# Two blocks of mixed layers on one core: both parts of x in one 512-column matmul

## The chip, the core and the metric

The kernel runs on one core of one Trainium2 chip. The metric is the device time of one execution in microseconds, the median of several runs. TensorE multiplies, VectorE (DVE), ScalarE (ACT) and GpSimd (POOL) do the rest, and SyncE (SP) issues the transfers from HBM.

## What is computed

Four layers over 256 tokens of 2048 features in float32. Each layer is a norm, a wide projection in, a token mixer, and a projection out that is added to the residual. Cut to what matters here:

```python
def even_layer(x, ...):                     # first block: attention beside S5
    proj = rmsnorm(x, norm_g) @ w_in        # 2048 -> 6144
    q, k, v, u, z_a, z_b = split(proj)
    o_a = chunked_relpos_attention(q, k, v, rel_bias) * silu(z_a)
    y = gelu(s5_ssm(u, ...))                # a recurrence over tokens, 64 groups
    o_b = y * sigmoid(y @ w_glu + b_glu) * silu(z_b)
    return x + concatenate([o_a, o_b]) @ w_out
def odd_layer(x, ...):                      # attention with forget gates
    q, k, v, z, f = split(rmsnorm(x, norm_g) @ w_in)
    return x + (forgetting_attention(q, k, v, f) * silu(z)) @ w_out
# second block, even layer: HGRN2 beside sparse attention, its two halves
# joined @ w_out (4096 -> 2048); odd layer: a short convolution and a gated
# linear recurrence of 2560 features; a norm at the end of each block
```

Nearly all the arithmetic is the products with the weights. They are made from float32 numbers that are each cut in two parts, a rounded one ("hi") and the rest ("lo"): x·w is taken as hi·hi + hi·lo + lo·hi.

## The kernel before, in words

**Stream of weights.** `Kern.run` (line 267) walks over a list of jobs. A job is 1024 columns of weights in one tile: `issue` (276) has SP load it (`raw`, 512 KB, five buffers), `prep` (285) has ACT round it to `hi` and DVE take `lo` = raw − hi (four buffers each), and the job's matmuls follow on TensorE. `ahead` (313) splits the weights of the next two jobs before a job's matmuls are written down.

**Groups.** `Kern.group` (359) makes the jobs of 512 output features. In the orientation 'W' a job holds two blocks of 128 input features (k-tiles) and all 512 columns. For each k-tile and each of its four blocks of 128 columns it emits three matmuls through `mmr` (line 420), each with a weight load of its own, into one 256-column sum (256 tokens):

```python
self.mmr(o_, wh, xh, s, False)
self.mmr(o_, wh, xl, False, False)
self.mmr(o_, wl, xh, False, l)
```

So a job is 8 such triples, 24 matmuls. The four sums of a group fill a PSUM tile of 1024 columns; there are two such tiles (`ps_main`). In the orientation 'X' (the values of the attentions) x is the stationary side and the matmuls have 512 columns. `Act` (27) holds x for four k-tiles; `Act.split` (37) writes its hi and lo parts into two slots of 1024 columns, by one ACT and one DVE operation (or four of 256 columns each where a gain is multiplied in).

**What follows a group.** `post` functions empty the sums: `evac_scaled` multiplies by the norm's factor straight out of PSUM, `Layer.take` (1259) and `post_oa` add the sums of a projection out to the residual by one DVE operation of 1024 columns and split the result for the next layer. A `post` is put in `delayed` after its group's last matmul and written down in the next `bg_step`.

**Order of the work.** Everything that is not the weight stream (S5, the attentions, HGRN2, the norms) is written as generators in lanes. `bg_step` (234) lets each lane write down a step after each job, as long as a plan of the engines' busy time (`busy`, costs in `_ew`, `act`, `mm`; 2600 ns of clock for each job) says that no engine is over 3 us behind. Where a job needs something that is not yet written down, `run` calls `bg_step(force=True)` until it is: the steps then stand in the engines' queues with no job in between. Each engine works off its queue in order.

**The two places named below.** In the first layer (E1), `block(b)` in `s5` does the S5 recurrence for 8 blocks, two at a time: products into banks (bu), rotations and scans on DVE with two additions on POOL, the products of the outputs (y), the gelu, and after the fourth block of a half the split of `y[0]` or `y[1]`. The GLU's groups read `y[0]` in their first k-tiles and `y[1]` in their last. In the second block's even layer (E2) the 16 sparse attention heads end in `gate` (a POOL multiplication of 1024 columns) and the split of the last input of the projection out.

Of the kernel before, what the change touches and what calls it, by code (L numbers as in the profile page):

```python
# [26 lines left out]
class Act:  # L27
    """256 columns of tokens for `n` blocks of 128 features, as two float32r parts."""

    def __init__(self, K, src=None, n=4, scale=None, ready=False):  # L30
        self.K, self.src, self.n, self.scale, self.ready = K, src, n, scale, ready
        self.hi = self.lo = None
        self.uses = 0
        self.keep_src = False
        self.hook = None

    def split(self):
        if self.hi is not None:
            return
        assert self.ready  # L40
        K = self.K
        self.hi, self.lo = K.slot(F32R), K.slot(F32R)
        v = lambda t: t[:, :self.n * 256]
        if self.scale is None or isinstance(self.scale, float):
            sc = 1.0 if self.scale is None else self.scale
            K.act(v(self.hi), v(self.src), AF.Copy, scale=sc)
            if sc == 1.0:
                K.tt('D', v(self.lo), v(self.src), v(self.hi).bitcast(F32), OP.subtract)
            else:
                K.stt(v(self.lo), v(self.src), sc, v(self.hi).bitcast(F32), OP.mult, OP.subtract)  # L50
        else:
            for k in range(self.n):
                s = slice(k * 256, k * 256 + 256)
                K.act(self.hi[:, s], self.src[:, s], AF.Copy, scale=self.scale[:, k:k + 1])
                K.stt(self.lo[:, s], self.src[:, s], self.scale[:, k:k + 1],
                      self.hi[:, s].bitcast(F32), OP.mult, OP.subtract)
        if self.hook is not None:
            self.hook(self.src)
        if not self.keep_src:
            K.free_slot(self.src)  # L60
            self.src = None

    def used(self):
        self.uses -= 1
        if self.uses == 0:
            self.K.free_slot(self.hi)
            self.K.free_slot(self.lo)
            self.hi = self.lo = None


class Kern:
# [124 lines left out]
    def smax(self, out, a, b, acc):  # L196
        """out = -(a + b); acc = its least, the negative of the greatest of a + b"""
# [29 lines left out]
    def lane(self, gens, width=1, prio=0, name=""):  # L227
        """a queue of (condition, generator maker), `width` of them at a time"""
# [5 lines left out]
    def bg_step(self, force=False):  # L234
# [32 lines left out]
    def run(self):  # L267
        jobs = self.jobs
        units = []
        for j in jobs:  # L270
            units.append([(j['unit'][0][:, j['off']:j['off'] + j['n']], j['n']), None])
# [41 lines left out]
        def ahead(i):  # L313
            """the splits of the jobs after job i, as far as LOOK goes"""
# [44 lines left out]
    def group(self, name, src, acts, orient, post, units, ready=None, bg=False):  # L359
        """one group of 512 columns: `units` is the list of (DRAM AP, kt count)"""  # L360
        st = {}

        def ps():
            if 'ps' not in st:
                self.nslot += 1
                if bg:
                    self.banks.free -= 2
                    st['ps'] = [self.ps_bg.tile([128, 512], F32, name=f"b{self.nslot}{i}", tag="b") for i in range(2)]
                    st['half'] = st['ps']
                else:  # L370
                    p = st['ps'] = self.ps_main.tile([128, 1024], F32, name=f"mm{self.nslot}", tag="mm")
                    st['half'] = [p[:, :512], p[:, 512:]]
            return st['half']

        kt = 0
        total = sum(n for _, n in units)
        for u, n in units:
            key = (u, n * 512)
            for h in range(0, n, self.JK):
                w = min(self.JK, n - h)  # L380
                ks = list(range(kt + h, kt + h + w))
                al = []
                for k in ks:
                    if acts[k][0] not in al:
                        al.append(acts[k][0])
                for a in al:
                    a.uses += 1

                def mmf(hi, lo, ks=ks):
                    p = ps()  # L390
                    hv = hi.rearrange("p (k c) -> p k c", c=512)
                    lv = lo.rearrange("p (k c) -> p k c", c=512)
                    for i, k in enumerate(ks):
                        a, o = acts[k]
                        xh, xl = a.hi[:, o * 256:o * 256 + 256], a.lo[:, o * 256:o * 256 + 256]
                        f, l = k == 0, k == total - 1
                        if orient == 'W':
# [2008 lines left out]
```

## Time and profile before

| | |
|---|---|
| median of 3 runs | 2397.28 us (2393.36 to 2397.49) |
| span of the profiled execution | 2394.8 us (the page gives no other time of it) |
| PE busy, matmuls | 2336.9 us, 98% of the span, 19906 |
| weight loads busy | 2253.3 us, 94% |
| DVE busy | 1585.9 us, 66% |
| ACT busy | 1152.5 us, 48% |
| POOL busy | 386.8 us, 16% |
| DMA | 402 MB, 168 GB/s on average |

Busy time of PE is the time in which at least one matmul is in flight; matmuls overlap, so the pace is read from the starts of matmuls that follow each other, not from one matmul's length. The page's 40 slices show PE at nine tenths or more in all but the first and last, and the granted clock at its full 2.4 GHz but for a few short stretches. A "product" with two or three small matmuls of a lane on tile `b` stands at L219 or L224, those of the weight stream at L420; L165, L176 and L194 are helpers that record DVE operations, L214 records all of ACT.

### The profile page before, as it was taken

To read this page: it belongs to the slowest core of one execution; us is meant where nothing else is said; L and a number is where in the kernel's file an instruction comes from. 1 tells how busy PE (TensorE), PEld (TensorE's weight loads), DVE (VectorE), ACT (ScalarE), POOL (GpSimd) and SP (SyncE) were. 2 spreads that over 40 slices of the span, in tenths; PEclk is the share of its full clock that TensorE was granted. 3 is DMA by queue.
4 is the path that set the end of the run, shared out by engine and by line. 5 is a ranking of instruction groups with operands and counts; after the bars stand their busy time and mean duration, and the time that the engine had idled before them with its cause. 6 is when DMAs were issued, how large, how long until landed. Compare 5 with 4: busy or idle time off the path is not lost.

```text
span 2394.8 us, 47663 instructions
## 1 busy us (share of the span) xinstructions
PE 2336.9 (98%) x19906; PEld 2253.3 (94%) x19906; DVE 1585.9 (66%) x2409; ACT 1152.5 (48%) x1662; POOL 386.8 (16%) x320
## 2 busy tenths in 40 slices
PE   7999999999999999999999999999999999999997
PEld 7989998999999999989999999899999999999997
DVE  7978878675554545676758574566667446777764
ACT  5354454444444344543445443455555434666643
POOL 1111211010000000123324253101110000111210
PEclk9999999999999999999999999999999999999999
DMA  6544454555545555554544454554444555555453
GB/s 225 191 152 149 142 177 153 175 186 164 193 160 175 174 170 185 169 177 156 170 160 159 162 165 159 192 178 142 142 142 143 195 183 180 165 175 168 161 196 111
DMA packets 116167, 402.23 MB, mean 168 GB/s; under 512 B 14832, under 2 KB 17776, under 8 KB 115952
## 3 DMA queue, kind: packets, MB, share of 16 engines
q1 hardware_dynamic: 115952, 399.19, 50.7%
q8 instruction: 156, 2.56, 0.4%
q14 instruction: 59, 0.48, 0.1%
HBM read 396.00 MB, written 2.10 MB: 166 GB/s over the span
## 4 chain that ended last, share of the span: by engine, by line
PE 84%; DVE 8%; POOL 2%; issue 2%; ACT 2%; DMA 1%; DVEq 0%; SPq 0%; ACTq 0%; POOLq 0%
PE mm L420 75%; PE b L219 6%; DVE lo L165 3%; DVE s L165 2%; POOL s L165 2%; DVE s L194 1%; DVE s L176 1%; PE b L224 1%; PE b L420 1%; ACT s L214 1%; ACT hi L214 1%; DMA raw<-in_e_in 1%; PE b L1836 0%; DVE s L170 0%; DMA s<-in_e_bias 0%
## 5 line engine op out<-in xcount | busy, mean ns | idle before, releaser
L420 PE MATMUL mm<-s,hi 128*128 128x256 f32 x9984 | 1830.5, 285 | 10.4 <-ACT s L214 7.6
L420 PEld LDWEIGHTS mm<-s,hi 128*128 128x128 f32 x9984 | 1563.9, 193 | 18.3 <-ACT s L214 8.0
L420 PE MATMUL mm<-s,lo 128*128 128x256 f32 x4992 | 1418.6, 284 | 24.5 <-DVE lo L165 24.4
L165 DVE TENSOR_TENSOR lo<-raw,hi 128x1024 fp32r<-128x1024 f32 x730 | 934.0, 1294 | 622.2 <-ACT hi L214 620.4
L214 ACT ACTIVATE hi<-raw 128x1024 fp32r<-128x1024 f32 x730 | 756.9, 1054 | 646.1 <-PE mm L420 557.5
L420 PEld LDWEIGHTS mm<-s,lo 128*128 128x128 f32 x4992 | 960.8, 192 | 28.9 <-DVE lo L165 28.8
L165 POOL TENSOR_TENSOR s<-s,s 128x512 f32<-128x512 f32 (+1 forms) x128 | 273.9, 2154 | 1411.4 <-ACT s L214 586.9
L214 ACT ACTIVATE s<-s 128x1024 f32<-128x1024 f32 (+6 forms) x188 | 132.9, 713 | 263.3 <-DVE s L165 137.2
L420 PE MATMUL mm<-hi,s 128*128 128x512 f32 x768 | 244.6, 394 | 0.0
L219 PE MATMUL b<-s,s 128*32 128x32 f32 (+8 forms) x3008 | 175.0, 244 | 4.8 <-POOL s L186 2.1
L420 PEld LDWEIGHTS mm<-hi,s 128*128 128x128 f32 x768 | 145.0, 189 | 30.8 <-ACT s L214 0.3
L219 PEld LDWEIGHTS b<-s,s 128*32 128x32 f32 (+2 forms) x2976 | 148.3, 135 | 23.4 <-POOL s L186 2.5
L420 PE MATMUL mm<-lo,s 128*128 128x512 f32 x384 | 150.5, 392 | 1.6 <-DVE lo L165 1.6
L214 ACT ACTIVATE s<-b 128x384 f32<-128x384 f32 (+6 forms) x135 | 57.2, 462 | 134.9 <-PE b L219 92.7
L165 DVE TENSOR_TENSOR s<-s,s 128x512 f32<-128x512 f32 (+8 forms) x134 | 85.8, 666 | 45.7 <-ACT s L214 44.5
L420 PEld LDWEIGHTS mm<-lo,s 128*128 128x128 f32 x384 | 72.6, 189 | 16.7 <-DVE lo L165 2.4
L176 DVE SCALAR_TENSOR_TENSOR s<-s,s 128x1024 f32<-128x1024 f32 (+3 forms) x76 | 82.6, 1089 | 3.1 <-ACT s L214 2.2
L214 ACT ACT_TABLE_LOAD x44 | 56.5, 1283 | 16.1 <-DVE s L176 14.7
L204 DVE COPY_PREDICATED s<-hmask,b 32x64 f32<-32x64 int32 (+1 forms) x144 | 36.0, 250 | 30.4 <-PE b L219 26.6
L214 ACT ACTIVATE s<-s,nsam 128x15 f32<-128x15 f32 (+2 forms) x96 | 37.6, 394 | 36.0 <-DVE nsam L199 36.0
L170 POOL TENSOR_SCALAR s<-alibi 128x256 f32<-128x256 f32 x16 | 17.8, 1111 | 212.3 <-PE b L219 174.1
L186 POOL MEMSET s<- 128x512 f32 (+7 forms) x65 | 25.8, 410 | 123.3 <-DMA s<-in_e_bias 59.1
(148 smaller groups left out, 966.6 us busy)
## 6 DMA issues: line engine op xcount, KB each, us to landing
raw<-in_e_in SPq DMA_DIRECT2D x336, 512.0 KB, 4.1
raw<-in_o_in SPq DMA_DIRECT2D x208, 512.0 KB, 4.0
raw<-in_e_out SPq DMA_DIRECT2D x80, 512.0 KB, 4.2
raw<-in_o_out SPq DMA_DIRECT2D x72, 512.0 KB, 4.4
raw<-in_e_outa SPq DMA_DIRECT2D x16, 512.0 KB, 3.6
raw<-in_o_rg SPq DMA_DIRECT2D x10, 512.0 KB, 3.7
raw<-in_e_glu SPq DMA_DIRECT2D x8, 512.0 KB, 3.8
raw<-in_e_cmp SPq DMA_DIRECT2D x8, 512.0 KB, 5.1
```

What stands on the lines that cost most here:

```text
L165: self._eng(e).tensor_tensor(out, a, b, op=op)
L170: self._eng(e).tensor_scalar(out, a, s1, None, op0=op0)
L176: self.nc.vector.scalar_tensor_tensor(out, a, s, b, op0=op0, op1=op1)
L186: self._eng(e).memset(out, v)
L194: self.nc.vector.tensor_tensor_scan(out, d0, d1, init, op0=OP.mult, op1=OP.add)
L204: self.nc.vector.copy_predicated(out, mask, a)
L214: self.nc.scalar.activation(out, a, func, scale=scale, **kw)
L219: self.nc.tensor.matmul(out, l, r, start=start, stop=stop, skip_group_check=True, **kw)
L224: self.nc.tensor.transpose(out, a, self.ident[:p, :p])
L420: self.nc.tensor.matmul(out, l, r, start=start, stop=stop, skip_group_check=True)
```

## The change

In 'W' the hi and lo part of x for one k-tile now lie side by side in one slot (`Act.both`, 512 columns), and one 512-column matmul with the rounded weights makes hi·hi in columns 0 to 255 and hi·lo in columns 256 to 511 of a PSUM bank. The third product, lo·hi, is added to the second sum by a 256-column matmul. The two sums are added when they are taken out: by an ACT copy of one and a DVE addition of the other, 512 columns at a time, into a slot that the old `post` then reads; or, in a projection out, by two DVE additions to the residual. Since a sum now takes two times 256 columns, a PSUM tile holds 256 output features, and a 'W' group is written as two halves h of 256 columns, each over all k-tiles; a job is four k-tiles of 256 columns, 8 pairs, 16 matmuls. The gates of the last layer (orientation 'B') keep the three matmuls. The layouts in HBM are cut accordingly; number and size of the loads stay.

```diff
     def group(...)
+        hs = 2 if orient == 'W' else 1
+        per = total * hs // len(jobs)
...
+        def total_of(h):
+            p = st[h].rearrange("p (c x t) -> p x c t", c=2, x=2)
+            if h == 0:
+                if self.slots.free < 3:
+                    return 'wait'
+                st['t'] = self.slot()
+            t = flat(st['t'][:, h * 512:h * 512 + 512], 2)
+            self.act(t, p[:, 1], AF.Copy)
+            def gen():
+                yield
+                self.tt('D', t, p[:, 0], t, OP.add)
+                if h == 1:
+                    yield
+                    while post(st['t']) == 'wait':
+                        yield 'wait'
+            self.lane([(lambda: True, gen)], prio=0, name="total")
...
-                            for c in range(4):
-                                o_ = p[c // 2][:, c % 2 * 256:c % 2 * 256 + 256]
-                                wh, wl = hv[:, i, c * 128:c * 128 + 128], lv[:, i, c * 128:c * 128 + 128]
-                                s = f and c % 2 == 0
-                                self.mmr(o_, wh, xh, s, False)
-                                self.mmr(o_, wh, xl, False, False)
-                                self.mmr(o_, wl, xh, False, l)
+                        for c in range(2):
+                            o_ = p[:, c * 512:c * 512 + 512]
+                            w = slice(c * 128, c * 128 + 128)
+                            self.mmr(o_, hv[:, i, w], a.both(o), f, False)
+                            self.mmr(o_[:, 256:512], lv[:, i, w], a.hi(o), False, l)
...
+    def last_late(self, n):
+        j = self.jobs[-2 * n:]
+        self.jobs[-2 * n:] = j[:n - 1] + j[n:2 * n - 1] + [j[n - 1], j[2 * n - 1]]
...
-    def take(self, g, ps, xr):
-        K.tt('D', xr, ps, xr, OP.add)
-        a.split()
+    def take(self, g, h, ps, xr):
+        add_both(self.K, xr, h, ps)
+        a.split((h,))
...
+def add_both(K, xr, h, p):
+    x = flat(xr[:, h * 512:h * 512 + 512], 2)
+    K.tt('D', x, p[:, 1], x, OP.add)
+    K.tt('D', x, p[:, 0], x, OP.add)
```

`Act.split` works on two parts of 512 columns, each of them a slot with two k-tiles. `last_late` puts the last job of each half behind the others in a layer's first group and in the first group of a projection out. Of the GLU's 8 jobs the order is now 0, 2, 1, 3, 4, 6, 5, 7: both halves of the first group, then of the second (before: the k-tiles of `y[0]` of both groups, then those of `y[1]`).

The change moves the background steps against the jobs. PE at the end of E1's S5: the products of the last block's outputs (tile b, with s5's rows), and the jobs around them. In the kernel before:

```order
L420 MATMUL mm_4592<-s_3854,lo_4632 128x256
L219 MATMUL b_4664<-s_858,s_4622 128x128
L219 MATMUL b_4664<-s_4138,s_4622 32x128 x4
L219 MATMUL b_4664<-s_4139,s_4622 32x128 x8
L219 MATMUL b_4664<-s_4138,s_4622 32x127 x4
L219 MATMUL b_4664<-s_4139,s_4622 32x127 x8
L420 MATMUL mm_4774<-s_3665,hi_4673 128x256
L420 MATMUL mm_4774<-s_3666,hi_4673 128x256
L420 MATMUL mm_4774<-s_3665,lo_4674 128x256
```

And in the changed one, from the second products of that block on:

```order
L235 MATMUL b_4136<-s_879,s_3879 128x128 x4
L471 MATMUL mm_4151<-s_2817,hi_4055 128x512
L471 MATMUL mm_4151<-s_2817,lo_4056 128x256
L471 MATMUL mm_4151<-s_2820,hi_4055 128x512
L471 MATMUL mm_4151<-s_2820,lo_4056 128x256
...
L235 MATMUL b_4207<-s_4198,s_3880 32x32 x8
L235 MATMUL b_4207<-s_824,s_4198 128x128
L235 MATMUL b_4207<-s_4015,s_4198 32x128 x4
...
L235 MATMUL b_4207<-s_4015,s_4198 32x127 x4
L471 MATMUL mm_4083<-s_4256,hi_4077 128x512
L471 MATMUL mm_4083<-s_4256,lo_4078 128x256
```

Before, the last block's outputs were followed by the last group of `outa` (four jobs on the attention's output, mm_4774) and four GLU jobs on `y[0]` before `y[1]` was read. Now one job (mm_4151, the second on `y[0]`, 16 matmuls) stands between the block's input products (b_4136) and its outputs (b_4207), and the very next matmul (mm_4083) reads s_4256, the first part of `y[1]`.

DVE at the same place, in the changed kernel, from the rotations of that last block to the split of `y[1]` (lo_ is a job's weights; s_4256 and s_4259 are the parts of `y[1]`):

```order
L181 TENSOR_TENSOR s_4015<-b_4135,s_3880 128x512
L181 TENSOR_TENSOR s_4016<-b_4136,s_3880 128x512
L181 TENSOR_TENSOR lo_4174<-raw_3988,hi_4173 128x1024
...
L210 SCALAR_TENSOR_TENSOR s_4015<-s5mag_101,s_4015 128x128 x8
L192 SCALAR_TENSOR_TENSOR s_4016<-s_4015,s_3880 128x512
L181 TENSOR_TENSOR s_4015<-s_4015,s_3880 128x512 x2
L181 TENSOR_TENSOR s_4198<-b_4207,s5row_103 128x128
L192 SCALAR_TENSOR_TENSOR s_3880<-s_824,s5d_99,b_4207 128x256
L188 TENSOR_SCALAR s_3880<-s_3880 128x256
L192 SCALAR_TENSOR_TENSOR s_4256<-s_3242,s_4256 128x2x256
L192 SCALAR_TENSOR_TENSOR s_4259<-s_3242,s_4259 128x2x256
```

In the kernel before, twelve `lo` of jobs stood between the same operations; now one does, so the chain stands by itself.

PE at the end of E2's last attention head, where the last input of the projection out is made. Before:

```order
L219 MATMUL b_20348<-s_20277,s_16781 128x256
L219 MATMUL b_20348<-s_20102,s_16778 128x128
L219 MATMUL b_20348<-s_20102,s_16947 128x128
L420 MATMUL mm_19902<-s_20286,hi_20282 128x256
L420 MATMUL mm_19902<-s_20287,hi_20282 128x256
```

And now:

```order
L235 MATMUL b_17173<-s_17137,s_14045 128x256
L235 MATMUL b_17173<-s_16973,s_14042 128x128
L235 MATMUL b_17173<-s_16973,s_14211 128x128
L471 MATMUL mm_16605<-s_17187,hi_17103 128x512
L471 MATMUL mm_16605<-s_17187,lo_17104 128x256
```

Before, four jobs on earlier inputs (s_20286 and the next) came between the head's last product and the first matmul on the last input; now s_17187, which is the last input, is read at once.

## Rows read from the trace of the kernel before

**Rows 1.** The page: engines' busy us (share) xinstructions; costliest groups, busy us, mean ns.

```profile
PE 2336.9 (98%) x19906; PEld 2253.3 (94%) x19906; DVE 1585.9 (66%) x2409; ACT 1152.5 (48%) x1662; POOL 386.8 (16%) x320
...
L420 PE MATMUL mm<-s,hi 128*128 128x256 f32 x9984 | 1830.5, 285 | 10.4 <-ACT s L214 7.6
...
L420 PE MATMUL mm<-s,lo 128*128 128x256 f32 x4992 | 1418.6, 284 | 24.5 <-DVE lo L165 24.4
L165 DVE TENSOR_TENSOR lo<-raw,hi 128x1024 fp32r<-128x1024 f32 x730 | 934.0, 1294 | 622.2 <-ACT hi L214 620.4
L214 ACT ACTIVATE hi<-raw 128x1024 fp32r<-128x1024 f32 x730 | 756.9, 1054 | 646.1 <-PE mm L420 557.5
```

**Rows 2.** Timeline of PE, 'W': start us, us, engine, line, operation, tiles, shapes, count.

```profile
800.07 0.40 PE L420 MATMUL mm<-s,hi 128*128 128x256 f32 x2
800.31 0.28 PE L420 MATMUL mm<-s,lo 128*128 128x256 f32 x1
800.43 0.40 PE L420 MATMUL mm<-s,hi 128*128 128x256 f32 x2
```

**Rows 3.** Timeline of PE in an 'X' group.

```profile
1510.46 0.62 PE L420 MATMUL mm<-hi,s 128*128 128x512 f32 x2
1510.91 0.39 PE L420 MATMUL mm<-lo,s 128*128 128x512 f32 x1
1511.14 0.62 PE L420 MATMUL mm<-hi,s 128*128 128x512 f32 x2
```

**Rows 4.** Waits: who waited for whom: us in total, times, longest.

```profile
DVE lo L165 <- ACT hi L214: 620.4, 348, 10.2
ACT hi L214 <- PE mm L420: 557.5, 300, 6.2
...
PE mm L420 <- DVE lo L165: 26.0, 21, 2.6
```

**Rows 5.** Groups by form: busy us, mean ns; idle before, what ended it.

```profile
L165 POOL TENSOR_TENSOR s<-s,s 128x1024 f32<-128x1024 f32 x44 | 122.3, 2783 | 1077.7 <-ACT s L214 586.9 <-DVE s L176 436.6 <-DVE s L194 54.2
...
L165 DVE TENSOR_TENSOR s<-mm,s 128x1024 f32<-128x1024 f32 x19 | 23.2, 1222 | 8.4 <-PE mm L420 8.4
...
L165 DVE TENSOR_TENSOR s<-b,s 128x512 f32<-128x512 f32 x32 | 20.3, 676 | 0.1
...
L214 ACT ACTIVATE s<-b 128x512 f32<-128x512 f32 x20 | 12.0, 598 | 46.2 <-PE b L219 46.1
...
L165 DVE TENSOR_TENSOR s<-s,s 128x512 fp32r<-128x512 f32 x3 | 2.1, 685 | 0.0
...
L214 ACT ACTIVATE s<-s 128x512 fp32r<-128x512 f32 x3 | 1.9, 628 | 0.0
```

**Rows 6.** Windows: length, busy us of PE, PEld, DVE, ACT, POOL; clock, DMA share.

```profile
0.00:420.00 420.00, 397.02 (x3512) 378.68 (x3513) 348.55 (x678) 197.95 (x337) 76.83 (x97) 0.98 0.52 170
...
2040.00:2280.00 240.00, 228.38 (x1869) 226.20 (x1868) 185.63 (x191) 156.26 (x208) 46.37 (x16) 0.99 0.51 169
```

**Rows 7.** Chain that ended last, where S5 ends: start us, us, what.

```profile
403.97 2.10 PE b L219 x66
406.07 13.99 PE mm L420 x115
```

**Rows 8.** Timeline of DVE, S5's last blocks.

```profile
353.52 1.28 DVE L165 TENSOR_TENSOR s<-b,s 128x512 f32<-128x512 f32 x2
...
384.57 1.36 DVE L194 TENSOR_TENSOR_SCAN s<-s5mag,s 128x128 f32<-128x128 f32 x4
...
389.56 0.68 DVE L176 SCALAR_TENSOR_TENSOR s<-s,s 128x512 f32<-128x512 f32 x1
...
393.43 1.28 DVE L165 TENSOR_TENSOR s<-s,s 128x512 f32<-128x512 f32 x2
...
409.51 0.43 DVE L165 TENSOR_TENSOR s<-s 128x256 f32<-128x256 f32 x1
```

**Rows 9.** Timeline of POOL there.

```profile
375.43 2.21 POOL L165 TENSOR_TENSOR s<-s,s 128x512 f32<-128x512 f32 x1 [4.70 <-DVE s L165]
```

More of the change, by code (lines that the diff above doesn't have):

```diff
@@ L31, in __init__ @@
         self.K, self.src, self.n, self.scale, self.ready = K, src, n, scale, ready
-        self.hi = self.lo = None
+        self.parts = [None, None]
+        self.whole = False
         self.uses = 0
@@ L35, in __init__, with both @@
         self.hook = None
-    def split(self):
-        if self.hi is not None:
-            return
[L40 to L56, printed above, removed]
+    def both(self, k):
+        return self.parts[k // 2][:, k % 2 * 512:k % 2 * 512 + 512]
@@ new lines, in hi, with lo, split @@
+    def hi(self, k):
+        return self.both(k)[:, 0:256]
+    def lo(self, k):
+        return self.both(k)[:, 256:512]
+    def split(self, halves=(0, 1)):
+        K = self.K
+        for s in halves:
+            if self.parts[s] is not None:
+                continue
+            assert self.ready or len(halves) == 1
+            t = self.parts[s] = K.slot(F32R)
+            if self.scale is None or isinstance(self.scale, float):
+                sc = 1.0 if self.scale is None else self.scale
+                v = t.rearrange("p (k h c) -> p h k c", h=2, c=256)
+                x = flat(self.src[:, s * 512:s * 512 + 512], 2)
+                K.act(v[:, 0], x, AF.Copy, scale=sc)
+                if sc == 1.0:
+                    K.tt('D', v[:, 1], x, v[:, 0].bitcast(F32), OP.subtract)
+                else:
+                    K.stt(v[:, 1], x, sc, v[:, 0].bitcast(F32), OP.mult, OP.subtract)
+            else:
+                for k in (2 * s, 2 * s + 1):
+                    x = self.src[:, k * 256:k * 256 + 256]
+                    K.act(self.hi(k), x, AF.Copy, scale=self.scale[:, k:k + 1])
+                    K.stt(self.lo(k), x, self.scale[:, k:k + 1], self.hi(k).bitcast(F32), OP.mult, OP.subtract)
+        if self.whole or None in self.parts:
+            return
+        self.whole = True
@@ L65, in used @@
         if self.uses == 0:
-            self.K.free_slot(self.hi)
-            self.K.free_slot(self.lo)
-            self.hi = self.lo = None
+            for t in self.parts:
+                self.K.free_slot(t)
 class Kern:
@@ L357, in run, with group, ps @@
             assert n < 5000, [(l['name'], len(l['q']), len(l['live'])) for l in self.lanes]
-    def group(self, name, src, acts, orient, post, units, ready=None, bg=False):
+    def group(self, name, acts, orient, post, jobs, ready=None, half=None):
+        total = len(acts)
+        hs = 2 if orient == 'W' else 1
+        per = total * hs // len(jobs)
         st = {}
-        def ps():
-            if 'ps' not in st:
+        def ps(h):
+            if h not in st:
                 self.nslot += 1
-                if bg:
+                if orient == 'B':
@@ L1283, in ready @@
             return xr[g] is not None
-        K.group(f"{tag}.out{g}", None, acts, 'W', post,
-                [(D[wname][g * n + i], 4) for i in range(n)], ready=ready)
+        K.group(f"{tag}.out{g}", acts, 'W', None, [D[wname][g * 2 * n + i] for i in range(2 * n)], ready=ready, half=half)
+        if g == 0:
+            K.last_late(n)
 def attend(K, S_mm, bias, pv, out, left, done, heads=2):
@@ L1885, in nsa @@
         for x, n in reversed(list(enumerate(('kc', 'vc')))):
-            keys = [(D['e2_cmp'][2 * x + u], 2048) for u in range(2)]
             for u in (1, 0):
@@ L2166, in fin @@
             return gen
-        keys = [(D['o2_rg'][u], 2048) for u in range(5)]
         def gates(i):
@@ L2172, in gates @@
                 o = (b % 2) * 2
-                K.group(f"o2.rg{b}", None, [(self.xc[i], o), (self.xc[i], o + 1)], 'W', post_gate(b), [(D['o2_rg'][i], 2)], bg=True)
-                n = 2 // K.JK
-                for m in range(n):
-                    K.jobs[m - n].update(unit=keys[i], off=(b % 2) * 1024 + m * 512)
+                K.group(f"o2.rg{b}", [(self.xc[i], o), (self.xc[i], o + 1)], 'B', post_gate(b), [D['o2_rg'][b]])
         seq = ['x0', 'x1', 'r0', 'g0', 'x2', 'r1', 'g1', 'x3', 'r2', 'g2', 'x4', 'r3', 'g3', 'r4', 'g4']
@@ L2308, in layout @@
     w = I['w_in_odd'][0]
[L2309 removed]
+    D['o1_in'] = units(w, [n * 2048 + 512 * i for i in range(4) for n in range(4)], 'WWXW' * 4)
     D['o1_f'] = narrow(w[:, 8192:], 32)
```

190 lines of the change are left out of this document (98 added, 92 removed).

## The prediction, made before the changed kernel ran

> **What bounds the kernel now.** I read the page first: matmuls are in flight for 98% of the span, and two groups of 9984 and 4992 matmuls of 256 columns stand far ahead of all others [rows 1]. They are the 4992 triples of the 'W' groups. Being in flight says nothing of the pace, so the timeline comes next: three of them start within 0.36 us, 120.0 ns each [rows 2]. Then the waits, to see whether something else sets that pace: VectorE's splits of weights wait 620 us for ScalarE's, and ScalarE's wait 558 us for matmuls to give a buffer back, while matmuls wait for VectorE's splits only 26 us in all [rows 4]. So the splits run ahead and are held back by TensorE; TensorE's own pace is the bound nearly everywhere. The exceptions are found in the windows: VectorE is busy for 349 of the first 420 us and for 186 of the 240 us from 2040 on [rows 6]. The chain shows the first place from inside: S5's last products start at 403.97, straight into a run of jobs [rows 7].
>
> **What the pair costs.** The change turns a triple into a pair: one matmul of 512 columns and one of 256. The nearest row for the long one is the 'X' group, which also loads new weights for every matmul: three starts in 0.68 us, 226.7 ns each [rows 3]. Between 120.0 and 226.7 lie 256 columns, so a column costs 0.417 ns and a matmul 13.3 ns besides. The pair should take 226.7 + 120.0 = 346.7 ns against 360.0. The short one still has to cover the load for the long one, as each 256-column matmul covers one now, and that holds the 120 today. 4992 × 13.3 ns = **66.6 us less**. Bounds: no gain if the pair went at 360, and none beyond 346.7, since both matmuls have rows of their own at their pace.
>
> The Trainium skill (TensorE: Matmul & The Clock Gate, Back-to-back issue gap) puts a warm matmul at N/2.4 + 2.5 ns. That would make triple and pair differ by 2.5 ns alone, 12.5 us in all. The rows give 13.3 ns for the fixed part, so the trace disagrees, and the sum goes by the rows.
>
> **What it adds elsewhere.** 58 'W' groups now pass through an addition: 116 ACT copies of 512 columns out of PSUM and 116 DVE additions, by the nearest rows 0.598 and 0.676 us [rows 5], 69 and 78 us. The 20 groups that go to a residual take four DVE additions of 512 columns, 2.70 us, in place of one of 1024 at 1.22 [rows 5]: 20 × 1.48 = 30 us. Splits in two parts cost 0.685 twice on DVE [rows 5] where one of 1024 columns costs about as much as a `lo`, 1.29 [rows 1]: some 3 us. Together about 110 us on DVE and 75 on ACT, which raises DVE from 66% to some 71%. Loads, POOL's work and the other matmuls stay as they are. All this lies beside the matmuls as long as the splits keep their lead of two jobs, and the 620 us of waiting for ScalarE say that DVE has the room [rows 4]. For what leaks through in the two dense stretches I charge 4 us, between 0 and the 26 us that PE waits for DVE today.
>
> Then the places where the order has changed, each worked out as a chain less its cover:
>
> *S5's end in E1.* The lanes fall back by the added DVE work, and the plan now reaches the GLU before S5 is done. From the last block's input products to `y[1]` the chain is: four multiplications out of banks, 2 × 1.28; POOL's second addition, 2.21 [rows 9]; eight scans, 2 × 1.36; then 0.68, 0.68 and 1.28 for the second rotation [rows 8], in all 10.1. One `lo`, 1.3 [rows 1], and four small steps of the block before, at 0.43 each [rows 8] 1.7, stand between. The output products take at most the 2.1 that they took at 403.97, with 66 of them there [rows 7]. The gelu is five such small steps, 2.2, and the split in two parts 0.63 + 0.63 + 0.69 [rows 5], 1.9. That is 19.3 us, against one job of 8 pairs in between, 2.8 us. Before, the same chain ran under jobs, and eight more jobs followed before `y[1]` was read. **16.5 us more.** It can be some 5 less if parts overlap, and 15 more if DVE comes to the place with a backlog, or if the gap lets TensorE's clock fall from 2.4 to 1.2 GHz for a while, as it does for parts of the first 420 us (0.98 on average) [rows 6].
>
> *GLU into E1's projection out.* The second GLU group is now last as a whole; copy 0.60, addition 0.68, four tanh steps at about 0.43, the product 1.3 and the split 1.9 are 6.2 us, 8.3 with ScalarE's rounding of two jobs ahead of them, and two jobs, 5.5 us, cover it: 3 us, at the upper end.
>
> *PSUM handed on.* With `last_late` the first half of a layer's first group ends one job before its tile is wanted again. The copy, one rounding, one `lo` and the addition (0.60 + 1.05 + 1.29 + 0.68 = 3.6) [rows 1, 5] stand against 2.8: 0.9 us, in three layers, 3 us.
>
> *E2's end.* The last head's products are followed at once by the job that reads them: copy about 0.4, POOL's gate 2.78, split 1.95 [rows 5], some 5.3 us, where four jobs, 11.5 us, covered it before.
>
> At the start the fourth block of x is wanted after three jobs and not six, but its loads stand in the same place among the others; I take 0, give or take 3. The last group's end is shorter by about 1 us, also left at 0.
>
> **The sum.** −66.6 + 4 + 16.5 + 3 + 3 + 5.3 = −34.8. From the span of 2394.8 that is 2360.0. The median of the runs is 2.5 us above that span, which may be the time around the span or chance; with it, **2362 us**.
>
> **Rivals.** *Nothing shows* (14%): the chains at S5's end and E2's end hide after all, because the steps counted as serial overlap, or the jobs run later than reckoned. Then 2397.3 − 66.6 + 4 = 2335. For it: DVE idles 71 us of the first 420 [rows 6]. Against: the order leaves one job between the products.
>
> *The ends cost double* (10%): each of the chains doubles through waiting lines on DVE. 2362 + 32 = 2394, hardly better than before. DVE at 83% in E1 speaks for it [rows 6].
>
> *The pair saves nothing* (5%): the change does not do what it says if the short matmul cannot cover the load for the long one. Then only the costs are left: 2397.3 + 32 = 2429. Rows 2 and 3 speak against it, each with one load for each matmul. A fixed part of 2.5 ns, as the Trainium skill's page named above has it, would give 2417 instead; the rows do not bear it out.
>
> *VectorE becomes the bound in E1 and in the last layer* (7%), the case on the other side. In E1 12 groups' additions and 8 residuals add 16 + 12 = 28 us of DVE, in the stretch from 2040 on ten groups add 13.5. If these stretches follow DVE one for one, they grow by 41.5 and the triples in them (960 and 640, 21.3 us) gain nothing; with the 32 us of the ends: 2397.3 − 66.6 + 21.3 + 41.5 + 32 = 2426. It decides when more than 43 of DVE's 71 idle us in E1 cannot be filled, because DVE waits there for what comes before it. The chain's share of PE speaks against it.
>
> **The numbers.** The forecast, with the sum off by up to some 17 us either way, has 64%. About 5 us, 0.2%, is what a measurement tells from no change. Faster: 64 + 14 and six of the ten for the double ends, 84%; same 4%; slower 12%. The range goes from 2334, which takes in the first rival, to 2388, at which most of the doubled ends are in; what is left out is about 2 in 10.
>
> **What would show it.** In the profile after: 4992 matmuls of 512 and 4992 of 256 columns in 'W', a 512 start 120 ns after the last 256 and the next 227 ns later; if the sum of two starts is 360, the pair's price is wrong. In the chain, a stretch of 15 to 20 us of S5's steps on DVE and POOL with PE idle between two GLU jobs, and some 5 us of POOL and ACT at the end of E2; if PE is dense there, the first rival is right. Waits of PE for `lo` far above 26 us, in the first 420 us or from 2040 on, would mean that DVE has become the bound. The forecast is wrong if the time lies under 2345 or over 2380.

## The result and the profile after

The changed kernel takes 2425.16 us (median of 4 runs, 2422.79 to 2427.28) against 2395.36 us for the kernel before in the same comparison. The ratio is 1.0127, with a 95% interval of 1.0113 to 1.0141: some 30 us slower, where 35 us faster were forecast. The profiled execution has a span of 2420.8 us, 26.0 more than that of before.

In this code the matmuls of the stream stand at L471, the lanes' small products at L235 and L240, ScalarE at L230, VectorE's helpers at L181, L192 and L210. From the page of the changed kernel, busy times and the costliest groups:

```profile
PE 2315.8 (96%) x14914; PEld 1990.7 (82%) x14914; DVE 1698.8 (70%) x2610; ACT 1211.5 (50%) x1803; POOL 387.3 (16%) x320
...
PEclk9999999899999999999999999999999999999999
...
L471 PE MATMUL mm<-s,hi 128*128 128x512 f32 x4992 | 1801.5, 404 | 36.6 <-DVE s L192 17.8
L471 PE MATMUL mm<-s,lo 128*128 128x256 f32 x4992 | 1411.1, 283 | 18.5 <-DVE lo L181 18.4
L181 DVE TENSOR_TENSOR lo<-raw,hi 128x1024 fp32r<-128x1024 f32 x730 | 957.4, 1323 | 559.2 <-ACT hi L230 556.4
...
L181 DVE TENSOR_TENSOR s<-mm,s 128x512 f32<-128x512 f32 x196 | 134.5, 686 | 27.4 <-PE mm L471 25.4
```

Against [rows 1]: as many pairs as there were triples, 113 us more of VectorE (about 110 had been reckoned), 59 more of ScalarE (75). The idle time ahead of the matmuls has grown, and it no longer ends mainly with a `lo`. The waits of the changed kernel say the same (who waited for whom, us in all, times, longest):

```profile
DVE lo L181 <- ACT hi L230: 556.4, 348, 11.2
...
PE mm L471 <- DVE lo L181: 19.2, 22, 2.1
PE mm L471 <- DVE s L192: 17.8, 5, 7.8
PE mm L471 <- DVE s L181: 16.1, 8, 4.3
```

The splits of weights still run ahead, as in [rows 4]; TensorE waits for them 19.2 us instead of 26.0. What is new is that it waits for VectorE's work on activations (`s`). Of the 17.8 us, 7.8 are the first wait of the kernel, which was 7.3 us before, on ScalarE; the rest is new.

Where the time went is read best by layer. The jobs of a layer are the same in number in both kernels, so their matmuls can be counted off (16, 12 or 24 to a job) and the same point of the work compared. The marks are the first job of E1 and of the second layer (O1); E2 is marked one job behind its first and the last layer eleven jobs behind its first (at the first jobs themselves the differences between the runs below are the same to about 1 us). The windows between the marks as busy times, for the kernel before (length, then busy us of PE, PEld, DVE, ACT, POOL, granted clock, DMA share, GB/s):

```profile
0.00:488.80 488.80, 464.49 (x4068) 445.55 (x4069) 392.92 (x720) 234.22 (x385) 81.65 (x99) 0.99 0.52 171
488.80:983.20 494.40, 492.18 (x3729) 471.73 (x3728) 274.87 (x359) 223.51 (x305) 29.67 (x14) 1.00 0.54 175
983.20:2019.10 1035.90, 1030.61 (x9249) 989.40 (x9248) 655.57 (x1058) 486.38 (x709) 219.36 (x181) 1.00 0.50 164
2019.10:2394.80 375.70, 349.63 (x2868) 346.64 (x2866) 262.52 (x276) 208.41 (x264) 56.13 (x26) 0.98 0.50 164
```

And for the changed one:

```profile
0.00:522.20 522.20, 466.45 (x3108) 397.44 (x3109) 419.51 (x773) 246.81 (x416) 82.75 (x99) 0.96 0.51 160
522.20:1009.70 487.50, 484.63 (x2697) 416.26 (x2696) 303.91 (x400) 237.49 (x334) 27.22 (x14) 1.00 0.57 177
1009.70:2054.90 1045.20, 1022.81 (x7119) 879.26 (x7119) 694.67 (x1122) 510.19 (x766) 224.19 (x181) 0.99 0.52 163
2054.90:2420.80 365.90, 341.92 (x1996) 297.74 (x1994) 280.69 (x316) 217.03 (x290) 53.09 (x26) 0.98 0.53 167
```

E1 loses 33.4 us, the second layer (O1) gains 6.9, E2 loses 9.4, the last layer gains 9.9. In E1 VectorE is busy for 80% of the time, in O1 for 62%. TensorE's idle time is the length less PE: it grows from 24.3 to 55.8 us in E1 and from 5.3 to 22.4 in E2.

The last layer's gain is not mainly the pair's. Before, TensorE waits there for `lo` (2020 to 2290 us):

```profile
PE mm L420 <- DVE lo L165: 11.9, 10, 2.0
```

In the changed kernel, in the same part of the work (2055 to 2320 us):

```profile
PE mm L471 <- DVE lo L181: 6.8, 7, 2.1
```

In the run three256 below, which does not have the pair, these waits are 4.9 us, and from this mark to the end it takes 7.8 us less than the kernel before.

The pair's pace is the next thing to look at. Two stretches of the changed kernel's PE timeline, at 800 us and at 1150 us:

```profile
800.08 0.28 PE L471 MATMUL mm<-s,lo 128*128 128x256 f32 x1
800.20 0.39 PE L471 MATMUL mm<-s,hi 128*128 128x512 f32 x1
800.43 0.28 PE L471 MATMUL mm<-s,lo 128*128 128x256 f32 x1
...
801.12 0.28 PE L471 MATMUL mm<-s,lo 128*128 128x256 f32 x1
...
1149.82 0.28 PE L471 MATMUL mm<-s,lo 128*128 128x256 f32 x1
1149.94 0.40 PE L471 MATMUL mm<-s,hi 128*128 128x512 f32 x1
1150.17 0.28 PE L471 MATMUL mm<-s,lo 128*128 128x256 f32 x1
...
1150.88 0.28 PE L471 MATMUL mm<-s,lo 128*128 128x256 f32 x1
```

Three pairs take 1.04 us in the first stretch and 1.06 in the second. Over the uninterrupted stretches of six pairs or more two paces stand out, 346.7 and 353.3 ns a pair, kept to the end of the stretch (of some 200, 58 have the one and 110 the other; the remainder lie in between). The mean of all pairs below 400 ns is 351.0; the same mean for the triples before is 359.7. So a pair is 8.7 ns cheaper, not 13.3.

Last, the two ends that the prediction had named. S5's end on PE:

```profile
426.78 0.28 PE L471 MATMUL mm<-s,lo 128*128 128x256 f32 x1
437.17 0.44 PE L235 MATMUL b<-s,s 128*32 128x32 f32 x16 [10.10 <-ACT s L230]
438.01 4.36 PE L235 MATMUL b<-s,s 128*128 128x128 f32 x66 [0.40 <-DVE s L181]
445.90 0.50 PE L471 MATMUL mm<-s,hi 128*128 128x512 f32 x1 [3.54 <-DVE s L192]
```

For 19.1 us no matmul of the stream starts, where 16.5 had been forecast. The 66 products take 4.36 us and not the 2.10 of [rows 7]. The window of that stretch and the ones at E2's end show the clock:

```profile
430.00:440.00 10.00, 2.43 (x42) 2.02 (x46) 6.15 (x13) 1.85 (x6) 1.56 (x3) 0.50 0.02 9
440.00:450.00 10.00, 6.46 (x62) 5.27 (x52) 5.19 (x8) 2.90 (x5) 0.00 (x0) 0.68 0.02 3
1830.00:1840.00 10.00, 9.12 (x47) 8.40 (x48) 9.59 (x19) 4.96 (x10) 2.84 (x1) 0.72 0.22 61
1870.00:1880.00 10.00, 7.00 (x50) 6.34 (x48) 3.38 (x4) 2.38 (x5) 2.34 (x1) 1.00 0.55 180
1880.00:1890.00 10.00, 8.71 (x35) 7.57 (x36) 4.79 (x7) 3.71 (x6) 0.00 (x0) 0.66 0.17 52
```

After each of these gaps TensorE works for a while at 1.2 GHz (0.50), and pays a second time. Over the whole execution, before and now:

```profile
core 0: 2394.8 us, clock 0.995
core 0: 2420.8 us, clock 0.983
```

The traces show two levels only, 2.4 and 1.2 GHz. By the unrounded means TensorE is at the lower one for 26 us before and for 80 us now; what has been added lies in E1 (44 us against 14) and E2 (24 against 0). An estimate from these figures is that it costs 27 us at most, half of the difference, if matmuls were in flight all the time. At E2's end the chain of waits is the one forecast, POOL's gate, one rounding, one difference:

```profile
1877.50 2.35 POOL s L181
...
1879.88 0.64 ACT s L230
...
1880.54 0.70 DVE s L181
```

TensorE is idle for 4.3 us there; 5.3 had been reckoned. But a second gap of 6.45 us stands 50 us earlier, at 1824 us, inside an attention head (a transposition of its weights, then VectorE, then its products); that one no step of the prediction had. The timeline shows what held it up:

```profile
1823.40 1.04 PE L240 MATMUL b<-ident,s 128*128 128x128 f32 x8
...
1825.71 1.22 DVE L181 TENSOR_TENSOR s<-s,rsh 128x1024 f32<-128x1024 f32 x1
1826.96 1.06 ACT L230 ACTIVATE s<-s 128x1024 f32<-128x1024 f32 x1 [3.76 <-DVE s L181]
...
1828.87 1.12 ACT L230 ACTIVATE s<-b 128x512 fp32r<-128x512 f32 x3
```

The transposed weights lie in their bank from 1824.4 on. ScalarE comes to them only at 1828.87: first it stands for 3.76 us at a step of another group, whose sum VectorE scales at 1825.71.

### The profile page after: what moved, and what is told of

It is laid out like the page before. It is cut to its first block, busy times and chain, and to the rows that moved or that the text cites. A ratio compares the mean times of both kernels' runs of the same rounds, so it can differ in the third digit from the quotient of the medians.

```text
span 2420.8 us, 38056 instructions
## 1 busy us (share of the span) xinstructions
PE 2315.8 (96%) x14914; PEld 1990.7 (82%) x14914; DVE 1698.8 (70%) x2610; ACT 1211.5 (50%) x1803; POOL 387.3 (16%) x320
## 4 chain that ended last, share of the span: by engine, by line
PE 77%; DVE 12%; issue 5%; ACT 4%; POOL 2%; DMA 0%; DVEq 0%; ACTq 0%; SPq 0%; POOLq 0%
PE mm L471 68%; PE b L235 6%; DVE lo L181 5%; DVE s L181 4%; ACT s L230 2%; ACT hi L230 2%; POOL s L181 2%; DVE s L192 1%; PE b L471 1%; PE b L240 1%; DVE s L210 1%; DVE s L188 0%; PE b L1889 0%; PE mm L235 0%; ACT L230 0%
## 5 line engine op out<-in xcount | busy, mean ns | idle before, releaser
L471 PE MATMUL mm<-s,hi 128*128 128x512 f32 x4992 | 1801.5, 404 | 36.6 <-DVE s L192 17.8
L471 PE MATMUL mm<-s,lo 128*128 128x256 f32 x4992 | 1411.1, 283 | 18.5 <-DVE lo L181 18.4
L181 DVE TENSOR_TENSOR lo<-raw,hi 128x1024 fp32r<-128x1024 f32 x730 | 957.4, 1323 | 559.2 <-ACT hi L230 556.4
L471 PEld LDWEIGHTS mm<-s,hi 128*128 128x128 f32 x4992 | 947.8, 190 | 266.9 <-DVE s L192 19.2
L471 PEld LDWEIGHTS mm<-s,lo 128*128 128x128 f32 x4992 | 953.6, 191 | 27.4 <-DVE lo L181 26.4
L230 ACT ACTIVATE hi<-raw 128x1024 fp32r<-128x1024 f32 x730 | 759.1, 1054 | 429.8 <-PE mm L471 370.2
L181 POOL TENSOR_TENSOR s<-s,s 128x512 f32<-128x512 f32 (+1 forms) x128 | 271.7, 2136 | 1454.6 <-ACT s L230 882.8
L230 ACT ACTIVATE s<-s 128x1024 f32<-128x1024 f32 (+5 forms) x214 | 136.0, 649 | 277.6 <-DVE s L181 148.1
L471 PE MATMUL mm<-hi,s 128*128 128x512 f32 x768 | 244.4, 393 | 0.6 <-ACT hi L230 0.6
L235 PE MATMUL b<-s,s 128*32 128x32 f32 (+9 forms) x3008 | 179.6, 248 | 27.6 <-ACT s L230 10.1
L235 PEld LDWEIGHTS b<-s,s 128*32 128x32 f32 (+2 forms) x2976 | 150.5, 137 | 57.5 <-issue 18.8
L471 PEld LDWEIGHTS mm<-hi,s 128*128 128x128 f32 x768 | 144.2, 188 | 32.1 <-ACT hi L230 1.0
L181 DVE TENSOR_TENSOR s<-mm,s 128x512 f32<-128x512 f32 x196 | 134.5, 686 | 27.4 <-PE mm L471 25.4
L471 PE MATMUL mm<-lo,s 128*128 128x512 f32 x384 | 149.8, 390 | 0.8 <-DVE lo L181 0.8
L230 ACT ACTIVATE s<-mm 128x512 f32<-128x512 f32 (+1 forms) x118 | 69.4, 589 | 159.0 <-PE mm L471 156.0
L230 ACT ACTIVATE s<-b 128x384 f32<-128x384 f32 (+6 forms) x135 | 57.2, 462 | 121.7 <-PE b L235 94.9
L181 DVE TENSOR_TENSOR s<-s,s 128x512 fp32r<-128x512 f32 (+7 forms) x160 | 85.3, 568 | 32.0 <-ACT s L230 30.7
L471 PEld LDWEIGHTS mm<-lo,s 128*128 128x128 f32 x384 | 72.1, 188 | 15.2 <-DVE lo L181 1.1
L192 DVE SCALAR_TENSOR_TENSOR s<-s,s 128x1024 f32<-128x1024 f32 (+3 forms) x78 | 81.1, 1042 | 1.1
L230 ACT ACTIVATE s<-s,nsam 128x15 f32<-128x15 f32 (+2 forms) x96 | 37.6, 394 | 35.5 <-DVE nsam L215 35.5
L202 POOL MEMSET s<- 128x512 f32 (+8 forms) x65 | 25.7, 408 | 175.0 <-DVE s L181 66.8
```

What stands on the lines that cost most here:

```text
L181: self._eng(e).tensor_tensor(out, a, b, op=op)
L192: self.nc.vector.scalar_tensor_tensor(out, a, s, b, op0=op0, op1=op1)
L202: self._eng(e).memset(out, v)
L230: self.nc.scalar.activation(out, a, func, scale=scale, **kw)
L235: self.nc.tensor.matmul(out, l, r, start=start, stop=stop, skip_group_check=True, **kw)
L471: self.nc.tensor.matmul(out, l, r, start=start, stop=stop, skip_group_check=True)
```

## The experiments

All runs stand in one table. The four columns on the right give the start of the layer (and the end) against the kernel before, in us of the profiled executions. Each is read from one execution; those of the changed kernel differ by 4.5 us among themselves, so two or three us in these columns can be chance.

| run | median us | ratio to before, interval | O1 at 488.8 | E2 at 983.2 | last at 2019.1 | end 2394.8 |
|---|---|---|---|---|---|---|
| changed kernel | 2425.16 | 1.0127 (1.0113–1.0141) | +33.4 | +26.5 | +35.9 | +26.0 |
| three256 | 2449.58 | 1.0220 (1.0204–1.0235) | +34.6 | +36.8 | +61.5 | +53.7 |
| seq4 | 2414.51 | 1.0074 (1.0058–1.0089) | +31.4 | +21.2 | +28.2 | +18.0 |
| blind | 2423.18 | 1.0106 (1.0086–1.0126) | +40.9 | +34.4 | +44.0 | +30.4 |
| blind_noadd | 2387.99 | 0.9968 (0.9957–0.9979) | +23.1 | +12.6 | +9.1 | −8.2 |
| noadd | 2390.50 | 0.9981 (0.9972–0.9991) | +19.8 | +9.7 | +6.7 | −4.9 |
| e1_triples | 2380.74 | 0.9936 (0.9920–0.9952) | −7.9 | −15.4 | −4.9 | −14.8 |
| e1e2_triples | 2368.91 | 0.9888 (0.9873–0.9903) | −9.1 | −16.6 | −17.0 | −28.2 |
| e1e2_seq4 | 2360.54 | 0.9854 (0.9838–0.9871) | −9.2 | −20.5 | −25.1 | −36.6 |
| e1e2_seq16 | 2360.95 | 0.9859 (0.9842–0.9875) | −8.3 | −20.6 | −24.7 | −36.2 |
| e1e2_bank | 2370.11 | 0.9898 (0.9883–0.9913) | −6.2 | −14.2 | −13.8 | −23.6 |

**three256: what the pair itself brings.**

```diff
-    self.mmr(o_, hv[:, i, w], a.both(o), f, False)
+    self.mmr(o_[:, 0:256], hv[:, i, w], a.hi(o), f, False)
+    self.mmr(o_[:, 256:512], hv[:, i, w], a.lo(o), False, False)
     self.mmr(o_[:, 256:512], lv[:, i, w], a.hi(o), False, l)
```

> The changed kernel with each 512-column matmul written as two of 256 columns, everything else in the same place. Theory A (the pair saves less than 13.3 ns: the starts in the changed kernel's trace give 351 ns a pair against 360 a triple, so 8.7 ns, 43 us over 4992): slower than the changed kernel by 35 to 43 us, about 2464 us (ratio to the kernel before about 1.029). Theory B (the pair saves 13.3 ns as predicted, and the chains cost 30 us more than A thinks): slower by 60 us or more, 2485 us. Theory C (the pair saves nothing): 2425 us.

Measured: 24.4 us slower than the changed kernel by the medians, 27.7 by the spans. None of the three amounts; A is nearest, and C falls. By layer the table tells why it is less than A said. The pair brings 1.2 us in E1, 9.1 in O1, 15.3 in E2 and 2.1 in the last layer; divided by the 960, 1032, 2128 and 872 pairs between the marks that is 1.3, 8.8, 7.2 and 2.4 ns. In O1 it is the 8.7 of the starts. In the first and the last layer, where VectorE is busy for 80 and 77% of the windows above, a cheaper matmul shows next to nothing. In E1 the starts show 351 ns there too, but TensorE is idle for 55.8 us, against 47.2 in three256: what the pair saves, TensorE waits longer. The rest of the change then costs 53.7 us, not 31.8.

The Trainium skill (TensorE: Matmul & The Clock Gate, Back-to-back issue gap) gives a fixed part of 2.5 ns for the gap of a single matmul at full clock. An estimate from it is that the pair saves 2.5 ns; in O1 the runs show 8.8, so the trace disagrees here too, though by less than with the 13.3 that I took from single rows.

**seq4: the order of the four matmuls of two pairs.**

```diff
 for c in range(2):
     self.mmr(o_, hv[:, i, w], a.both(o), f, False)
+for c in range(2):
     self.mmr(o_[:, 256:512], lv[:, i, w], a.hi(o), False, l)
```

> The changed kernel with the four matmuls of two pairs in another order: both of 512 columns, then both of 256. In the changed kernel's trace some stretches go at 346.7 ns a pair and others at 353.3 for as long as they last. Theory A (the slower pace belongs to the turn from a 512-column to a 256-column matmul and back): two pairs take 693 ns everywhere, 4.3 ns a pair less than the mean of 351, 4992 x 4.3 = 21 us faster than the changed kernel, about 2404 us. Theory B (the pace depends on something else, such as reads by other engines): within 4 us of 2425 us.

Measured: 10.6 us faster than the changed kernel, 8.0 by the spans; between the two. Two pairs now mostly take 696 ns, 348 a pair. In PE's timeline of seq4 (a row holds two matmuls; the first two rows stand right behind a small product and take 0.78 us, the next two 0.70):

```profile
799.79 0.71 PE L474 MATMUL mm<-s,hi 128*128 128x512 f32 x2
800.34 0.40 PE L474 MATMUL mm<-s,lo 128*128 128x256 f32 x2
800.57 0.63 PE L474 MATMUL mm<-s,hi 128*128 128x512 f32 x2
801.04 0.39 PE L474 MATMUL mm<-s,lo 128*128 128x256 f32 x2
801.27 0.40 PE L474 MATMUL mm<-s,hi 128*128 128x512 f32 x1
```

So the order matters to the pace. 346.7 was not reached, and why the alternating order has two paces stays open.

**blind, blind_noadd and noadd: the order of E1's steps, or VectorE's time?** Here the plan is not charged, with the helper `free()` that puts the planned times back:

```diff
-    self.act(t, p[:, 1], AF.Copy)
+    with self.free():
+        self.act(t, p[:, 1], AF.Copy)
...
-        self.tt('D', t, p[:, 0], t, OP.add)
+        with self.free():
+            self.tt('D', t, p[:, 0], t, OP.add)
...
-    K.tt('D', x, p[:, 0], x, OP.add)
+    with K.free():
+        K.tt('D', x, p[:, 0], x, OP.add)
```

> The changed kernel, but the plan of engine time that sets the order is not charged for the added copies and additions; they are all still done. Theory A (in E1 the background steps fall behind because of the plan, and TensorE then waits in S5's last chain): that chain is covered again, as no step has to be forced there; the stretch from the first GLU job to E1's projection out loses its 30 us, less some 8 us of new waits for the real work: about 2403 us. Theory B (VectorE itself is the bound in E1): the time stays lost, spread over E1 as waits of TensorE for split weights: within 5 us of 2425 us.

Measured: within 2 us of the changed kernel, the time that B gave, and E1 is 7.5 us worse. The gap at S5's end is gone, but gaps of 7.7, 5.1 and 13.5 us at 216, 315 and 383 us have come in its place. They end with steps of ScalarE and VectorE on activations, while TensorE waits 7.3 us in E1 for split weights (5.6 in the changed kernel): B's mechanism does not show. An order that takes no notice of the additions only moves the waiting. The same order with VectorE's additions left out:

```diff
-        with self.free():
-            self.tt('D', t, p[:, 0], t, OP.add)
+        with self.free():
+            pass
...
-    K.tt('D', x, p[:, 1], x, OP.add)
```

> The kernel of the run blind, in the same order, but without VectorE's second step of each sum: the 116 additions after the copies and one of the two in each residual are left out, so the sums lack hi.hi in the projections in and hi.lo and lo.hi in the residuals. In E1 that takes away 24 + 16 additions of 0.68 us, 27 us of VectorE. Theory A (VectorE is the bound in E1): the second layer's first group, 41 us late in blind, starts 25 us earlier. Theory B (the order, the PSUM tiles and the storage of the sums make the steps wait, not VectorE's time): it starts at most 8 us earlier. Over the whole kernel A gives about 2395 us, B about 2412 us.

Measured: O1 starts 17.8 us earlier, between 8 and 25; the whole takes 2388.0 us, less than A gave. Less than half of E1's loss in this order goes with the additions. So I repeated it in the changed kernel's own order:

```diff
-    self.tt('D', t, p[:, 0], t, OP.add)
+    self._ew('D', 512)
...
-    K.tt('D', x, p[:, 1], x, OP.add)
+    K._ew('D', 512)
```

> The changed kernel in exactly its own order (the plan is still charged), but without VectorE's second step of each sum: the 116 additions after the copies and one of the two in each residual are left out, 156 steps of some 0.68 us, 106 us of VectorE, 27 of them in E1; so the sums lack a part. Theory A (in E1 VectorE's own time is the bound, as blind_noadd's 18 us suggest): the second layer's first group, 33 us late in the changed kernel, starts about 18 us earlier, at 15 us late, and S5's last chain shrinks; over the whole kernel 30 to 38 us less, about 2390 us. Theory B (in the changed kernel's own order the 33 us are the chain of S5's end, the GLU's chains and the slow clock behind them, whose steps are not the additions): at most 8 us earlier there, about 2410 us over the whole kernel.

Measured: 2390.5 us, the total of A; in E1 13.6 us, between A and B. S5's last chain did not shrink, against A. PE's timeline of noadd there:

```profile
418.77 0.28 PE L473 MATMUL mm<-s,lo 128*128 128x256 f32 x1
428.91 0.44 PE L235 MATMUL b<-s,s 128*32 128x32 f32 x16 [9.86 <-ACT s L230]
429.75 4.36 PE L235 MATMUL b<-s,s 128*128 128x128 f32 x66 [0.40 <-DVE s L181]
437.64 0.50 PE L473 MATMUL mm<-s,hi 128*128 128x512 f32 x1 [3.53 <-DVE s L192]
```

That is 18.9 us against 19.1: the gap belongs to the chain. What the additions cost in E1 stands elsewhere: 8.0 us up to the GLU, 4.1 in the projection out. By layer they cost 13.6, 3.2, 12.4 and 1.7 us, 30.9 in all. That is 29% of the 106 us that they take on VectorE, although VectorE has over 500 us of waiting for `hi`. An addition that is left out takes nothing from VectorE's queue, but it is also no longer a link between a sum and the steps that read it, and its PSUM tile comes free sooner; the run does not separate these. ScalarE's copies are still in it.

**e1_triples and e1e2_triples: the old form where VectorE or a chain binds.** A group whose name is in a list is written in triples, into one PSUM tile of four sums, with the old `post`s, the old order of the GLU and of E1's projection out; x keeps the new layout.

```diff
+TRIPLE = ('e1',)
...
+        if orient == 'W' and name.startswith(TRIPLE):
+            orient = 'T'
...
-                    if orient == 'B':
+                    if orient in 'BT':
+                        q = p if orient == 'B' else [p[:, :512], p[:, 512:]]
```

> The changed kernel with the first layer's groups, its GLU and its projection out as triples in their old order, all other layers in pairs. Theory A: the start of the second layer's first group moves from 33 us after the kernel before's to about the same time; the rest of the kernel keeps what it has: 2425 - 33 = 2392 us. Theory B (the loss in E1 is the slower x layout, its splits in two parts, and not the pairs' sums and order): the second layer still starts 15 us or more late, 2407 us or more.

Measured: 44 us faster than the changed kernel; O1 starts 41.3 us earlier than there and 7.9 us earlier than before; A had 33 and 0. B falls: the new layout of x costs nothing. (Of the 7.9 us, 4.9 are idle time of TensorE, 19.4 against 24.3, and it is at 1.2 GHz for 6.8 us against 13.7. Which part of the edit does it was not followed up.) The window from 395 us to E1's end in e1_triples is dense and at full clock:

```profile
395.00:480.90 85.90, 85.10 (x753) 84.27 (x752) 58.64 (x63) 44.70 (x61) 4.83 (x2) 1.00 0.55 175
```

```diff
-TRIPLE = ('e1',)
+TRIPLE = ('e1', 'e2.b', 'e2.out0')
```

> The kernel of the run e1_triples with triples also in E2's last eight groups in and in the first group of its projection out, whose gaps of 6.6 and 4.4 us of TensorE and slow clock behind them cost 20 us between 1776 and 1880 us of the kernel before. Theory A (the halves and the slot held for a sum delay the last heads there): both gaps are gone, 20 us back, less 640 pairs that gain nothing now (4 us): 2365 us. Theory B (the heads are late for another reason): one gap or both stay, 2376 us or more.

Measured: 11.8 us faster than e1_triples, 13.4 by the spans. Both gaps are gone, as A said (A's total was 4 us lower). ScalarE still stands 2.6 us at the other group's step in front of the head at the first of them, but TensorE has two jobs to go on with; in the changed kernel none stood between the head's transposition and its products. It shows that the form of these groups made the heads late, not which part of it: the slot that a half sum holds, or the added steps, were not taken apart.

**e1e2_seq4, e1e2_bank and e1e2_seq16: the pace once more.** The first joins e1e2_triples and seq4.

> The kernel of the run e1e2_triples with the four matmuls of two pairs in the order of the run seq4 (512, 512, 256, 256). In seq4 two pairs took 696 ns, 348 a pair, against a mean of 351: 3400 pairs are left, 3 ns each: 10 us faster than e1e2_triples, and faster than the kernel before by 1.5 to 2%. If the gain of seq4 came from E1 and E2's end alone, no difference to e1e2_triples.

Measured: 8.4 us faster than e1e2_triples, 1.5% faster than the kernel before, and the fastest of all. Its page shows the clock at nine tenths or more in every slice:

```profile
PEclk9999999999999999999999999999999999999999
```

The other two change only the order within a job, `for c` outside `for k` in one, eight long matmuls ahead of eight short ones in the other:

```diff
-for i, k in enumerate(ks):
-    for c in range(2):
+for c in range(2):
+    for i, k in enumerate(ks):
```

> The kernel of the run e1e2_triples with the pairs of a job in another order: four k-tiles into one PSUM bank, then four into the other, so that neighbouring pairs write the same bank. Theory A (the slower pace of 353.3 ns a pair comes with the change of bank from pair to pair): 346.7 ns everywhere, some 4.5 ns for 3400 pairs, 15 us faster than 2369. Theory B (it belongs to the turns between 512 and 256 columns): within 4 us of 2369 us.

```diff
+each = [(i, k, c) for i, k in enumerate(ks) for c in range(2)]
+for i, k, c in each:
+    self.mmr(p[:, c * 512:c * 512 + 512], hv[...], both, k == 0, False)
+for i, k, c in each:
+    self.mmr(p[:, c * 512 + 256:c * 512 + 512], lv[...], hi, False, k == total - 1)
```

> The kernel of the run e1e2_triples with the 16 matmuls of a job in another order: eight of 512 columns, then eight of 256. Theory A (each turn between the two lengths costs something, and only turns do): 226.7 and 120.0 ns inside a run of one length, 346.7 a pair or little more, 5 us faster than the run e1e2_seq4 at 2360.5 us, or more. Theory B (a 512-column matmul that follows another one with new weights takes 233 ns, as in seq4): 233 + 115 = 348 a pair, within 3 us of 2360.5.

Measured: e1e2_bank is at 2370.11, no different from e1e2_triples, with both paces still there, so the change of bank is not the cause. e1e2_seq16 is at 2360.95, no different from e1e2_seq4; eight long matmuls take 1.84 us (802.02 to 803.86), 230 ns each, and eight short ones 0.95, 119 each:

```profile
802.02 2.00 PE L484 MATMUL mm<-s,hi 128*128 128x512 f32 x8
803.86 1.11 PE L484 MATMUL mm<-s,lo 128*128 128x256 f32 x8
804.81 0.40 PE L484 MATMUL mm<-s,hi 128*128 128x512 f32 x1
```

In both cases the time was that of B. But the first B puts the slower pace down to the turns between the two lengths, and with a quarter of seq4's turns seq16 is no faster: the turns do not explain it either.

## Why the prediction was wrong

The forecast of 35 us less was wrong in sign, and the range missed the time by 37 us. By the runs the sum reads, in spans: −27.7 for the pair (three256), +30.9 for the additions (noadd), and the rest of the 53.7, +22.8, for the order, the ends and the clock: +26.0. The prediction had −66.6, +4 and +27.8. The rest is found by difference and still holds ScalarE's copies; between the marks it is +21.0, −1.0, +12.3 and −9.5 us, so its nearness to 27.8 is luck: E1 and E2 lost more than that, and the last layer gave back what no term had.

- *The pair, −66.6 against −27.7.* This is the largest miss. The prediction took "no gain if the pair went at 360, and none beyond 346.7" as bounds and then the better bound as the value. 346.7 exists, in some stretches; 353.3 is the more frequent. The mean saves 8.7 ns, 43 us. The other part of the miss is that the term was counted in all layers, E1 and the last one included; there it brought 3.3 us of the 15.9 that 8.7 ns would give for the 1832 pairs in their windows.
- *The additions, +4 against +30.9.* "All this lies beside the matmuls as long as the splits keep their lead" was the step that failed. The splits kept it: TensorE waits for `lo` even less than before. But a long wait of VectorE for `hi` only says that the splits have time. It does not say that the chains of activations have any, and these run through the same queue. The gap at 1824 us shows such a case, on ScalarE's queue behind VectorE's. It is 6.0 us long in noadd too, so the additions' own time does not make it; it belongs to the order of the steps.
- *S5's end, 16.5 against 19.1*, and *E2's gate, 5.3 against 4.3*: right in mechanism and nearly in size (the parts given for the gate add up to 5.1). At S5's end the miss is the output products, 5.2 us from first to last at 1.2 GHz where 2.1 had been taken. What was left out is that TensorE works at 1.2 GHz behind such a gap. The prediction had it among the things that could add to S5's end, not in the sum. From 1881.3 to 1890 us TensorE starts 35 matmuls; at the pace a little later (58 in 10 us) it would start some 50, so about 2.7 us are lost behind that one gap.
- *The small chains.* GLU into the projection out, 3: waits of 2.7 and 2.1 us, at 468.3 and 476.2. PSUM handed on, 3: in E2 the chain stands as forecast (copy, rounding, `lo`, addition) and costs 1.9 us at 1032.7; in the last layer the wait is 0.8.
- *E2's head at 1824 us*, 6.45 us and the slow clock behind it, was not in the sum. The prediction looked at the last head's end only.
- *The rivals.* The one on the other side, VectorE as the bound in E1 and the last layer, had 7% and gave 2426 us. Its mechanism is at most partly borne out: in these two layers the pairs gain next to nothing, and in E1 the additions cost 13.6 us. In the last layer they cost 1.7 us by noadd, and the waits for `lo` have fallen from 11.9 to 6.8 us: VectorE is not the bound there. Its total is luck, since the additions cost 15 us in these layers and not 41.5, but 12.4 in E2, which it did not count, and the pairs elsewhere gain less than it reckoned. Its sign, waits for `lo` far above 26 us, did not come. "Nothing shows" falls, both chains show. "The ends cost double" falls too: the two chains went from 16.5 and 5.3 to 19.1 and 4.3. "The pair saves nothing" falls with three256; that its 2429 us lie 4 us from the measured time is luck, as the pair's 28 us and the additions' 27 us beyond the forecast all but cancel.

## What to carry to other kernels

A price that is read at one place of a trace should be read at several; two matmuls, each at its pace among its own kind, need not keep it when they alternate. When work is added to an engine that "waits a lot", ask which of its steps wait: slack in the steps of one stream is no cover for chains that go through the same engine. And a change that pays in open stretches need not be made everywhere: left out of the first layer and of E2's end, and with its matmuls in the order of seq4, this one turned a loss of 30 us into a gain of 34. The pair itself is only a part of that: by the marks 9.2 us come in E1, which has the old triples, and 11.5 in the last layer, where it is worth some 2.

## What was unexpected of the hardware

A matmul of 512 columns and one of 256 in turn go at one of two paces, 346.7 or 353.3 ns, and most stretches keep theirs to the end. In the order 512, 512, 256, 256 it is 348. Neighbouring pairs in the same PSUM bank make no difference (2370.1 us against 2368.9), and fewer turns between the two lengths make none either (2361.0 against 2360.5). The cause was not found.
